# A transformer layer on one Trainium2 core: gate pieces one by one and context decays among the levels in the GLA heads, and column turns, squares and factors at other places in the opening

## The chip, the cores and the metric

The kernel runs on one core of one Trainium2 chip. The metric is the device time of one execution in microseconds (us), the median over runs on the chip. Before the change it is 1982.68 us in three runs (1981.75 to 1982.88).

Five engines take part: PE (TensorE, the matrix products), ACT (ScalarE), DVE (VectorE), POOL (GpSimd) and SP (SyncE, which only issues DMAs here). Each has its own instruction stream in a fixed order, and they wait for one another through semaphores.

## The reference, cut to what matters

One hybrid layer over 256 latent tokens and 256 context tokens, width 2048, all float32. Only what the change touches is shown: the modulated norm, the one input projection, and the gated linear attention (GLA) with 4 heads of key width 256 and value width 512.

```python
mod_x = jnp.split((silu(c) @ w_mod + b_mod), 6); mod_c = jnp.split((silu(c_ctx) @ w_mod + b_mod), 6)
h  = rms_norm(x, g_mix) * (1 + mod_x[1]) + mod_x[0]
hc = rms_norm(ctx, g_mix) * (1 + mod_c[1]) + mod_c[0]
qa, ka, va, qb, kb, vb, rb, lrf, lrb, gate_a, gate_b = split(h @ w_in)     # and of hc
gf = log_sigmoid(lrf @ w_gate_f + b_gate_f) / 16                           # gb likewise
...
def gla_final_state(k, v, g):                 # of the context, forward and flipped
    b = cumsum(g, axis=1)
    return einsum("bthd,bthe->bhde", k * exp(b[:, -1:] - b), v)
def gla_chunked(q, k, v, g, s0):              # of the latent tokens, both directions
    ...                                       # o_t = q_t exp(b_t) s0 + sum_{s<=t} (q_t . k_s exp(b_t - b_s)) v_s
```

After these come attention over a window and the context, the merge of both branches, the output projection and a convolutional feed-forward part. The change leaves them alone.

## The kernel before, in words

**Products.** Every large float32 product is made of three products of a shorter type: a weight tile `raw` (128 x 1024) is copied to `whi` on ACT (L207), the rest `wlo` is a difference on DVE (L208), and PE takes hi·hi, lo·hi and hi·lo (L83). Weights stream in once, on SP's queue, 0.5 MB a tile.

**The opening.** The modulation columns (shift and scale of the first norm) must be there before the first projection. `mod_both` makes them for a group of k-tiles: each `step` loads a 1 MB tile `mraw` and multiplies it into `pm` on PE (L95), the last step's transpose `mtr` runs on DVE (L324), and `end` has a small product `pcol` on PE and copies on DVE (L334). So each `end` has PE wait for a transpose that itself waits for PE. The groups are (first k-tile, number): (0,2), (2,2), (4,4), (8,4), (12,4). `square_sums` and `factor_row` make the norms' row factors, on ACT, PE (`pr`, L448) and DVE. `affine_scale` multiplies x by factor and scale on DVE (L488), `affine_shift` adds the shift and splits into `h..hi` on ACT (L495) and `h..lo` on DVE (L496). Latent tiles begin with h0, context tiles with h1. For each group the projections QB, KB and VB of all tokens are then taken over that group's k-tiles; the sums of the groups gather in `qb0`, `kbt` and `vb0`. Group 0's QB columns go to `qb0` by ACT copies (L503). From group 1 on, `mid` is called inside the projections and takes as many steps of the next group's columns from `bg_steps` as the list `steps` says; a finished column's `end` goes through `put` to a queue that the next tick empties, or is run at once.

**The GLA heads.** `with_gla` runs `gla_A`, a generator, beside a block of projection products (VB columns; KB columns in head 0). The block has 8 k-tile pairs, and the generator is called twice in each, 16 calls to a head: one before the 16 hi·hi and lo·hi products of a pair, one before its 8 products with `wlo`. A rate (0.91) says after how many calls it goes on to its next `yield`. One head has:

- four gate pieces (two directions, two halves of the head): one product `pz` on PE, four ACT instructions (L721 to L725), one add on DVE for the latent half (L726) and one on POOL for the context half (`gc`, L727). They are two to a step;
- a product `pa` of raw queries and keys, then eight levels. Level lv takes exponentials on ACT (L766, L767, L773, L774), multiplies them into `q2` and `k2` on DVE (L768, L775), and updates four running sums `segs` on DVE (L777 to L780). The product of a level (`pa`, L95, then a DVE L751 `COPY_PREDICATED` into `at`) is placed one step behind, so that the next level's vector work runs meanwhile;
- at the end the products with the context's decayed keys. The decays `kf` and `kg` are four scans of `gc` on DVE (L800, L802), a total `tot`, three exponentials on ACT and two multiplies with the context keys on DVE (L808, L809), all behind level 7 in the program. The final `pa` takes them with `q2`, `q3`.

The order on each engine follows the order of the program, with a scheduler that moves DVE and ACT work within it by readiness; `in_order(a, b)` holds b behind a.

Of the kernel before, what the change touches and what calls it, by code (L numbers as in the profile page):

```python
# [8 lines left out]
F32 = mybir.dt.float32  # L9
# [3 lines left out]
ALU = mybir.AluOpType  # L13
# [18 lines left out]
def layer_kernel(ctx, tc, A, out):  # L32
# [363 lines left out]
    def rms_scale(ss, n, shape):  # L396
# [15 lines left out]
    mods = [[mod_both(part, t0, n, dst, put) for part, dst in ((1, scale1), (0, shift1))]  # L412
            for (t0, n), put in zip(groups, [None, None] + 3 * [lambda fn: defer(0, fn)])]

# [4 lines left out]
    def square_sums(s):  # L419
# [3 lines left out]
        for i in range(4):  # L423
            x_ = xr[2 * s + i // 2][:, (i % 2) * 4:(i % 2) * 4 + 4, :]
            q = wr.tile([P, 4, T], F32, name="sq", tag="raw")
            if s + i:
                S.activation(q, x_, AF.Square)
            else:
                V.tensor_tensor(q, x_, x_, op=ALU.mult)
                parts.extend(q[:, k, :] for k in range(4))  # L430
                continue
            h = q[:, 0:2, :]
            V.tensor_tensor(h, h, q[:, 2:4, :], op=ALU.add)
            if s and whole is not None:
# [114 lines left out]
    hold_hi.extend([None, j])  # L549
    proj_T(w_in, QB, kts, [h_all(0)], add_to(lambda i: qb0[i], True))  # L550
    proj_T(w_in, QB + 512, kts, [h_all(0)], add_to(lambda i: qb0[2 + i], True))
    wk, wv = wsplit_raw(raws[0]), wsplit_raw(raws[1])
# [12 lines left out]
    affine_shift(1, *groups[0])  # L565
    ea()
    b0()
    b1()
    for s in range(2):
        affine_scale(s, *groups[1])  # L570
    early.extend([wk, wv])
    proj_T(w_in, KB, kts, [h_all(1)], lambda i, b: S.activation(half(i, T), pair_of(b), AF.Copy), mid=eb)
    i0, j0 = affine_shift(0, *groups[1])
    proj_nat(w_in, 0, VB, kts, [h_tok(1, 0), h_tok(1, 1)],
             lambda i, b: S.activation(vb0[:, 2 + i, :], b, AF.Copy))
    early.extend(wload(w_in[2 * P:4 * P, c:c + 512]) for c in (QB, QB + 512, KB, VB))
    hold.append(i0)
# [18 lines left out]
    for gi, (t0, n) in enumerate(groups):  # L596
# [8 lines left out]
        if gi + 1 < len(groups):  # L605
            bg_steps.extend(mods[gi + 1][0] + mods[gi + 1][1])
            ticks = 4 * ((n + 1) // 2)
            bg_rate[:] = [1.4 * len(bg_steps) / ticks + 0.01, 0.0]
            if gi == 1:
                bg_rate[:] = [0.0, 0.0]  # L610
                steps = iter([1, 2, 1, 2, 2, 0])

                def mid():
                    pin[0] = last[0]
                    for _ in range(next(steps)):
                        bg_steps.pop(0)()
                    pin[0] = None
        if t0 == 8:
            more_h(1)
        for s in range(2):  # L620
            if gi > 1:
                affine_scale(s, t0, n)
                affine_shift(s, t0, n)
            if s == 0:
# [80 lines left out]
    def gla_A(h, kb, qb, res):  # L705
# [7 lines left out]
        for d in range(2):  # L713
            g_ = W2("fc", "gc", [P, 2, T])
            for dt in range(2):
# [10 lines left out]
                V.tensor_tensor((PF if d == 0 else SB)[:, dt, :], mn[:, 0:T], e[:, 0:T], op=ALU.add)  # L726
                G.tensor_tensor(g_[:, dt, :], mn[:, T:2 * T], e[:, T:2 * T], op=ALU.add)  # L727
            gc.append(g_)
            yield

# [26 lines left out]
        for lv in range(8):  # L757
# [21 lines left out]
            V.tensor_tensor(pfR, pfR, pfL[:, :, m - 1:m].to_broadcast([P, n, m]), op=ALU.add)  # L779
            V.tensor_tensor(sbL, sbL, sbR[:, :, 0:1].to_broadcast([P, n, m]), op=ALU.add)  # L780
            if lv == 1:
                yield
            if lv:
                products(lv - 1, *prev)
            prev = q2, k2
            yield
        products(7, *prev)
# [9 lines left out]
        tot = sm.tile([P, 2], F32, name="tot", tag="tot", bufs=2)  # L797
        one = ones[:, 0:1].to_broadcast([P, T])
        for dt in range(2):
            V.tensor_tensor_scan(kf[:, dt, :], one, gc[0][:, dt, :], 0.0, op0=ALU.mult, op1=ALU.add)  # L800
            V.memset(kg[:, dt, 0:1], 0.0)
            V.tensor_tensor_scan(kg[:, dt, 1:T], ones[:, 0:1].to_broadcast([P, T - 1]), gc[1][:, dt, 0:T - 1], 0.0,  # L802
                                 op0=ALU.mult, op1=ALU.add)
        V.tensor_scalar(tot, kf[:, :, T - 1], -1.0 / 16, None, op0=ALU.mult)
        for dt in range(2):
            S.activation(kf[:, dt, :], kf[:, dt, :], AF.Exp, scale=1.0 / 16, bias=tot[:, dt:dt + 1])
        S.activation(kg, kg, AF.Exp, scale=-1.0 / 16)
        V.tensor_tensor(kf, kf, kc, op=ALU.mult)  # L808
        V.tensor_tensor(kg, kg, kc, op=ALU.mult)  # L809
        yield  # L810
# [507 lines left out]
```

## Time and profile before

| what | value |
|---|---|
| median of three runs | 1982.68 us (1981.75 to 1982.88) |
| the profiled execution | 1981.3 us |
| its span (first to last instruction) | 1979.5 us |
| mean granted TensorE clock | 0.999 |
| PE busy | 1955.1 us, 99% of the span |
| DVE busy | 1399.8 us, 71% |
| ACT busy | 972.1 us, 49% |
| POOL busy | 44.2 us, 2% |

The profile is of one execution. A line of a timeline has the start, the length, the engine, the program line, the operation with output and inputs, and how many like it follow; in brackets, how long the engine stood idle before it and what released it. A line of waits has the engine and its line, the engine and line that released it, the total in us, how often, and the longest. A line of windows has a stretch, its length, and then the busy time of each engine in it, the clock, and the busy share and rate of the DMA engines. In the trace each product of the columns (`pm`) counts as two matmuls, so `x4` in the program's order reads `x8` there.

### The profile page before, as it was taken

How to read it: one execution, taken by the hardware profiler on the slowest of the kernel's cores; microseconds unless marked ns; L12 is line 12 of the kernel's file. 1: busy time of each engine (PE TensorE's matmuls, PEld its weight loads, DVE VectorE, ACT ScalarE, POOL GpSimd, SP SyncE). 2: the span in 40 equal slices, each digit the busy share in tenths (PEclk: the TensorE clock that was granted, in tenths of full speed). 3: DMA queues.
4: the chain of work that ended last, by engine and by line, in shares of the span. 5: the costliest groups of instructions: out<-in, count | busy, mean ns of one | idle time of the engine just before them, and what ended most of it. 6: DMA issues, size and time to landing. Idle time of an engine off the chain costs nothing.

```text
span 1979.5 us, 27075 instructions
## 1 busy us (share of the span) xinstructions
PE 1955.1 (99%) x10292; PEld 1636.0 (83%) x10292; DVE 1399.8 (71%) x2150; ACT 972.1 (49%) x1415; POOL 44.2 (2%) x60
## 2 busy tenths in 40 slices
PE   7999999999999999999999999999999999999999
PEld 5679988888887778888888888888888888888887
DVE  5756767876767988777766467989886555677754
ACT  4323555552345666444444445755555334555533
POOL 0010010012000000000000000000000000000000
PEclk9999999999999999999999999999999999999999
DMA  9966222336754456888888677688886566666563
GB/s 379 413 258 185 75 85 78 93 108 205 233 160 118 127 181 213 268 290 292 289 286 265 235 236 262 198 271 285 257 274 228 193 197 188 187 190 189 188 216 109
DMA packets 183666, 420.88 MB, mean 213 GB/s; under 512 B 12544, under 2 KB 12768, under 8 KB 178800
## 3 DMA queue, kind: packets, MB, share of 16 engines
q1 hardware_dynamic: 182000, 413.45, 63.9%
q0 software_dynamic: 1360, 5.54, 1.0%
q8 instruction: 80, 1.31, 0.3%
q14 instruction: 50, 0.41, 0.1%
q10 hardware_dynamic: 176, 0.17, 0.0%
HBM read 416.98 MB, written 2.13 MB: 212 GB/s over the span
## 4 chain that ended last, share of the span: by engine, by line
PE 68%; DVE 0%; ACT 0%; issue 0%; DVEq 0%
PE acc L83 52%; PE accs L83 12%; PE poa L95 1%; PE pS L95 1%; PE ptp L98 1%; PE pto L98 0%; PE ptx L98 0%; DVE wlo L208 0%; ACT s L986 0%; PE ptq L98 0%; DVE s L991 0%; DVE yd L1238 0%; DVE yd L1232 0%; DVE raw L365 0%; ACT whi L207 0%
## 5 line engine op out<-in xcount | busy, mean ns | idle before, releaser
L208 DVE TENSOR_TENSOR wlo<-raw,whi 128x1024 fp32r<-128x1024 f32 x568 | 694.1, 1223 | 439.9 <-ACT whi L207 396.4
L207 ACT ACTIVATE whi<-raw 128x1024 fp32r<-128x1024 f32 x568 | 601.5, 1060 | 765.9 <-PE acc L83 608.9
L83 PE MATMUL accs<-h,whi 128*128 128x512 f32 x704 | 176.3, 392 | 0.0
L83 PE MATMUL acc<-h,whi 128*128 128x512 f32 x640 | 160.4, 392 | 0.0
L83 PEld LDWEIGHTS accs<-h,whi 128*128 128x128 f32 x704 | 126.6, 189 | 22.7
L83 PE MATMUL acc<-whi,h01hi 128*128 128x512 f32 x352 | 139.9, 398 | 0.0
L83 PE MATMUL acc<-whi,h00hi 128*128 128x512 f32 x352 | 138.9, 395 | 0.0
L83 PE MATMUL acc<-whi,h00lo 128*128 128x512 f32 x352 | 138.1, 392 | 0.0
L83 PE MATMUL acc<-whi,h01lo 128*128 128x512 f32 x352 | 137.8, 392 | 0.0
L83 PE MATMUL acc<-whi,ah 128*128 128x512 f32 x352 | 137.0, 389 | 0.0
L83 PE MATMUL acc<-whi,al 128*128 128x512 f32 x352 | 137.0, 389 | 0.0
L83 PEld LDWEIGHTS acc<-h,whi 128*128 128x128 f32 x640 | 115.0, 189 | 20.6
L83 PEld LDWEIGHTS accs<-h,wlo 128*128 128x128 f32 x704 | 96.0, 190 | 6.9
L83 PE MATMUL acc<-wlo,h01hi 128*128 128x512 f32 x352 | 98.7, 396 | 0.0
L83 PE MATMUL accs<-h,wlo 128*128 128x256 f32 x704 | 98.2, 282 | 0.0
L83 PE MATMUL acc<-wlo,h00hi 128*128 128x512 f32 x352 | 97.8, 394 | 0.0
L83 PE MATMUL acc<-wlo,ah 128*128 128x512 f32 x352 | 94.3, 389 | 0.0
L83 PEld LDWEIGHTS acc<-h,wlo 128*128 128x128 f32 x640 | 87.4, 190 | 6.3
L83 PE MATMUL acc<-h,wlo 128*128 128x256 f32 x640 | 89.4, 282 | 0.0
L365 DVE CUSTOM_DVE_ANT_0 raw<-raw,csrow,pack 128x1024 f32<-128x1024 f32 x64 | 81.4, 1281 | 0.0
L83 PEld LDWEIGHTS acc<-whi,ah 128*128 128x128 f32 x352 | 66.1, 188 | 13.7
L83 PEld LDWEIGHTS acc<-whi,al 128*128 128x128 f32 x352 | 66.1, 188 | 13.7
(377 smaller groups left out, 3558.1 us busy)
## 6 DMA issues: line engine op xcount, KB each, us to landing
raw<-in_w_in SPq DMA_DIRECT2D x208, 512.0 KB, 4.2
raw<-in_w_up SPq DMA_DIRECT2D x176, 512.0 KB, 4.1
raw<-in_w_modT SPq DMA_DIRECT2D x128, 512.0 KB, 4.4
raw<-in_w_down SPq DMA_DIRECT2D x88, 512.0 KB, 3.6
mraw<-in_w_mod SPq DMA_DIRECT2D x32, 1024.0 KB, 12.1
raw<-in_w_attn_o SPq DMA_DIRECT2D x32, 512.0 KB, 5.0
raw<-in_w_gla_o SPq DMA_DIRECT2D x32, 512.0 KB, 5.1
raw<-in_w_out SPq DMA_DIRECT2D x32, 512.0 KB, 4.7
```

The source lines that it names most:

```text
L83: r = pe_seq(PE.matmul(*a, **k))
L95: return pe_seq(after(PE.matmul(*a, **k)))
L98: return pe_seq(after(PE.transpose(*a)))
L207: j = S.activation(hi[:, 0:n, :], raw[:, 0:n, :], AF.Copy).ins
L208: i = V.tensor_tensor(lo[:, 0:n, :], raw[:, 0:n, :], hi[:, 0:n, :].bitcast(F32), op=ALU.subtract).ins
L365: i0 = V.tensor_tensor_reduce(out=raws[i], in0=raws[i], in1=row[0], scale=1.0, scalar=d if h else bmod[:, b0:b0 + 1], op0=ALU.mult, op1=AL ...
```

## The change

There are two parts.

In the GLA heads, `gla_A` yields after each of the four gate pieces, the extra yield in level 1 is gone, and the rate is 0.97. The decays (the same scans, total, exponentials and multiplies) move from behind level 7 into the levels: one half's scans behind level 2, the other's behind level 3, total and exponentials behind level 4, the multiplies behind level 6, each held behind the last `segs` add of that level. `kf` and `kg` get their buffers from the tag `fb` instead of `fa`.

In the opening, two of the context's squares are held behind ACT's copies of QB group by group; group 1's scale column ends later (`ea` behind `b0` and `b1`), the context's scaling of group 1 stands behind the VB products of the context; group 2's column ends go to a list `pend` and are run one at a time at set calls of `mid`; its last four steps are taken in one call; and the scaling of group 2 and the latent shift are placed in the calls too.

```diff
@@ opening
-            for (t0, n), put in zip(groups, [None, None] + 3 * [lambda fn: defer(0, fn)])]
+            for (t0, n), put in zip(groups, [None, None] + [lambda fn: pend.append(fn)] + 2 * [lambda fn: defer(0, fn)])]
+    pend = []
...
-                S.activation(q, x_, AF.Square)
+                j = S.activation(q, x_, AF.Square).ins
+                if s and i in (0, 2):
+                    in_order(evicted[i + 1], j)
...
+    evicted = []
+    for j in range(2):
+        proj_T(w_in, QB + j * 512, kts, [h_all(0)],
+               lambda i, b, j=j: evicted.append(S.activation(qb0[2 * j + i], b, AF.Copy).ins))
...
-    ea()
     b0()
     b1()
-    for s in range(2):
-        affine_scale(s, *groups[1])
+    ea()
+    affine_scale(0, *groups[1])
...
+    affine_scale(1, *groups[1])
     early.extend(wload(w_in[2 * P:4 * P, c:c + 512]) for c in (QB, QB + 512, KB, VB))
...
-                steps = iter([1, 2, 1, 2, 2, 0])
+                steps = iter([1, 2, 1, 4, 0, 0])
+
+                def next_columns():
+                    if pend:
+                        pend.pop(0)()
+
+                def scale_2():
+                    next_columns()
+                    for s in range(2):
+                        affine_scale(s, *groups[2])
+
+                also = iter([next_columns] * 3 + [scale_2, next_columns, lambda: affine_shift(0, *groups[2])])
 
                 def mid():
                     pin[0] = last[0]
+                    next(also)()
                     for _ in range(next(steps)):
                         bg_steps.pop(0)()
...
-            if gi > 1:
+            if gi > 2:
                 affine_scale(s, t0, n)
+            if gi > 2 or (gi == 2 and s):
                 affine_shift(s, t0, n)
@@ gla_A
                 G.tensor_tensor(g_[:, dt, :], mn[:, T:2 * T], e[:, T:2 * T], op=ALU.add)
+                yield
             gc.append(g_)
-            yield
+
+        kf = W2("fb", "kf", [P, 2, T])
+        kg = W2("fb", "kg", [P, 2, T])
+
+        def decays(dt, level):
+            one = ones[:, 0:1].to_broadcast([P, T])
+            i = V.tensor_tensor_scan(kf[:, dt, :], one, gc[0][:, dt, :], 0.0, op0=ALU.mult, op1=ALU.add).ins
+            V.memset(kg[:, dt, 0:1], 0.0)
+            j = V.tensor_tensor_scan(kg[:, dt, 1:T], ones[:, 0:1].to_broadcast([P, T - 1]), gc[1][:, dt, 0:T - 1],
+                                     0.0, op0=ALU.mult, op1=ALU.add).ins
+            in_order(level, i, j)
+
+        def decayed(level):
+            tot = sm.tile([P, 2], F32, name="tot", tag="tot", bufs=2)
+            in_order(level, V.tensor_scalar(tot, kf[:, :, T - 1], -1.0 / 16, None, op0=ALU.mult).ins)
+            for dt in range(2):
+                S.activation(kf[:, dt, :], kf[:, dt, :], AF.Exp, scale=1.0 / 16, bias=tot[:, dt:dt + 1])
+            S.activation(kg, kg, AF.Exp, scale=-1.0 / 16)
+
+        def decayed_keys(level):
+            in_order(level, V.tensor_tensor(kf, kf, kc, op=ALU.mult).ins)
+            in_order(level, V.tensor_tensor(kg, kg, kc, op=ALU.mult).ins)
+
+        beside_levels = {2: lambda i: decays(0, i), 3: lambda i: decays(1, i), 4: decayed, 6: decayed_keys}
...
-            V.tensor_tensor(sbL, sbL, sbR[:, :, 0:1].to_broadcast([P, n, m]), op=ALU.add)
-            if lv == 1:
-                yield
+            level = V.tensor_tensor(sbL, sbL, sbR[:, :, 0:1].to_broadcast([P, n, m]), op=ALU.add).ins
             if lv:
                 products(lv - 1, *prev)
             prev = q2, k2
+            if lv in beside_levels:
+                beside_levels[lv](level)
             yield
...
-        kf = W2("fa", "kf", [P, 2, T])
-        kg = W2("fa", "kg", [P, 2, T])
...
-        V.tensor_tensor(kf, kf, kc, op=ALU.mult)
-        V.tensor_tensor(kg, kg, kc, op=ALU.mult)
@@ with_gla
-        beside[:] = [gla_A(h, kb, qbt, res), 0.91, 0.0]
+        beside[:] = [gla_A(h, kb, qbt, res), 0.97, 0.0]
```

What the change moves is seen best in the order of instructions on two engines. First PE, in the opening, at the end of group 1's KB products, where group 2's columns are made (`pm_4` and `pcol_4`; a number behind a name tells one buffer from the next). Before:

```order
L83 MATMUL acc<-h10hi,wlo 128x256
L83 MATMUL acc<-h00hi,wlo 128x256
L83 MATMUL acc<-h10hi,wlo 128x256
L95 MATMUL pm_4_673<-mraw,cS 32x512 x8
L95 MATMUL pcol_4_724<-mtr,pack 32x32
L83 MATMUL acc<-whi,h00hi 128x512
L83 MATMUL acc<-whi,h00lo 128x512
```

With the change, the place 16 `wlo` products earlier:

```order
L83 MATMUL acc<-h10hi,whi 128x256
L83 MATMUL acc<-h10lo,whi 128x256
L95 MATMUL pcol_4_666<-mtr,pack 32x32
L95 MATMUL pm_4_683<-mraw,cS 32x512 x16
L83 MATMUL acc<-h00hi,wlo 128x256
L83 MATMUL acc<-h10hi,wlo 128x256
L83 MATMUL acc<-h00hi,wlo 128x256
```

All four steps of the second column stand ahead of the 16 `wlo` products, and its `pcol` behind them; before, half of the steps and the `pcol` followed the products directly. The first column's `pcol` had stood 32 products further up, directly behind its own last `pm`.

Second PE, in head 1, where the gate pieces are. Before:

```order
L95 MATMUL pz<-wgl 128x512 x2
L83 MATMUL acc<-wlo,h00hi 128x512 x4
L83 MATMUL acc<-wlo,h10hi 128x512 x4
L95 MATMUL pz<-wgl 128x512 x2
L83 MATMUL acc<-whi,h00hi 128x512
```

With the change:

```order
L95 MATMUL pz<-wgl 128x512
L83 MATMUL acc<-wlo,h00hi 128x512 x4
L83 MATMUL acc<-wlo,h10hi 128x512 x4
L95 MATMUL pz<-wgl 128x512
L83 MATMUL acc<-whi,h00hi 128x512
```

The other two `pz` follow at the next two calls, behind the 16 `whi` and the next 8 `wlo` products; the first level product stands one call later than before, the products of levels 6 and 7 and the final one stand where they stood.

Third DVE, in the same head, at its end. Before:

```order
L794 TENSOR_TENSOR q_3133<-q_3133,qb 128x512
L62 TENSOR_TENSOR ats<-at,ats 128x256
L800 SCALAR_TENSOR_TENSOR kf<-ones,gc 128x256
L801 MEMSET kg 128x1
L802 SCALAR_TENSOR_TENSOR kg<-ones,gc 128x255
L62 TENSOR_TENSOR ats<-pa,ats 128x256
L800 SCALAR_TENSOR_TENSOR kf<-ones,gc 128x256
L801 MEMSET kg 128x1
L802 SCALAR_TENSOR_TENSOR kg<-ones,gc 128x255
L208 TENSOR_TENSOR wlo<-raw,whi 128x1024
L804 TENSOR_SCALAR tot<-kf 128x2
L809 TENSOR_TENSOR kg<-kg,kb_109 128x512
```

With the change the first two scans stand here, behind level 2:

```order
L821 TENSOR_TENSOR segs<-segs 128x64x4
L822 TENSOR_TENSOR segs<-segs 128x64x4
L793 COPY_PREDICATED at<-lmask,pa 128x256
L754 SCALAR_TENSOR_TENSOR kf<-ones,gc 128x256
L755 MEMSET kg 128x1
L208 TENSOR_TENSOR wlo<-raw,whi 128x1024
L756 SCALAR_TENSOR_TENSOR kg<-ones,gc 128x255
L810 TENSOR_TENSOR q_2955<-q_2955,qb 128x512
```

The scans, the total and the two multiplies (L768 and L769 now) have left the end of the head and stand ahead of DVE's work for levels 3, 4, 5 and 7. DVE's `wlo` and all other work keep their number.

More of the change, by code (lines that the diff above doesn't have):

```diff
@@ L549, in layer_kernel @@
     hold_hi.extend([None, j])
-    proj_T(w_in, QB, kts, [h_all(0)], add_to(lambda i: qb0[i], True))
-    proj_T(w_in, QB + 512, kts, [h_all(0)], add_to(lambda i: qb0[2 + i], True))
+    evicted = []
+    for j in range(2):
+        proj_T(w_in, QB + j * 512, kts, [h_all(0)],
+               lambda i, b, j=j: evicted.append(S.activation(qb0[2 * j + i], b, AF.Copy).ins))
     wk, wv = wsplit_raw(raws[0]), wsplit_raw(raws[1])
@@ L794, in gla_A @@
             V.tensor_tensor(dst, dst, q_, op=ALU.mult)
-        kf = W2("fa", "kf", [P, 2, T])
-        kg = W2("fa", "kg", [P, 2, T])
[L797 to L809, printed above, removed]
         yield
```

## The prediction, made before the changed kernel was run

> **What bounds the kernel now.** I read the page's totals first, then the waits of PE in the two places that the diff touches, then the timeline and the windows around each wait.
>
> ```profile
> span 1979.5 us, 27075 instructions
> PE 1955.1 (99%) x10292; PEld 1636.0 (83%) x10292; DVE 1399.8 (71%) x2150; ACT 972.1 (49%) x1415; POOL 44.2 (2%) x60
> ```
>
> PE is busy for all but 24.4 us of the span. The change removes no product, so it can only gain where PE waits, or where it starts late behind a wait. The first view is PE's waits from 24 to 75 us, the second the same from 205 to 460 us, the four GLA heads.
>
> ```profile
> PE pcol L95 <- DVE mtr L324: 2.6, 4, 0.8
> PE acc L83 <- ACT h10hi L495: 0.7, 1, 0.7
> PE acc L83 <- ACT h00hi L495: 0.4, 1, 0.4
> PE acc L83 <- ACT qb L503: 0.4, 1, 0.4
> PE acc L83 <- DVE h10lo L496: 0.2, 1, 0.2
> ```
>
> ```profile
> PE pa L95 <- DVE q L768: 3.1, 4, 1.1
> PE pa L95 <- DVE kf L808: 2.5, 3, 1.0
> ```
>
> All that can be had is there: 4.3 us in the opening, 5.6 us in the heads. A wait costs somewhat more than its row, because the last products before it run out unhidden. The rows of group 2's columns show it:
>
> ```profile
> 60.35 1.07 PE L95 MATMUL pm<-mraw,cS 128*32 128x512 f32 x8
> 62.26 0.25 PE L95 MATMUL pcol<-mtr,pack 128*32 128x32 f32 x2 [0.84 <-DVE mtr L324]
> ...
> 66.45 1.92 PE L95 MATMUL pm<-mraw,cS 128*32 128x512 f32 x16
> 68.30 0.39 PE L83 MATMUL acc<-h00hi,wlo 128*128 128x256 f32 x1
> ...
> 70.40 1.92 PE L95 MATMUL pm<-mraw,cS 128*32 128x512 f32 x16
> 73.16 0.25 PE L95 MATMUL pcol<-mtr,pack 128*32 128x32 f32 x2 [0.84 <-DVE mtr L324]
> 73.34 0.50 PE L83 MATMUL acc<-whi,h00hi 128*128 128x512 f32 x1
> ```
>
> Sixteen take 1.92 us and eight 1.07, so eight more cost 0.85: a group that is followed by a wait pays 1.07 - 0.85 = 0.22 us for its tail. The seven waits in the opening that the change touches (all but `h00hi`) are then worth at most 4.3 - 0.4 + 7 x 0.22 = 5.4 us, and the seven in the heads 5.6 + 7 x 0.22 = 7.1 us. That is the ceiling, 12.5 us.
>
> **The opening, part by part.** No arithmetic is added or removed. The edits and what each takes away: the context's squares behind ACT's QB copies lift the `qb` wait of 0.4 us; `ea` behind `b0` and `b1` puts 16 column products over the first of group 1's two `pcol` waits (2.6 - 2 x 0.84 = 0.9 us between them); the context's scaling of group 1 moved back frees DVE, and with it the `h10` waits of 0.7 and 0.2; group 2's ends, run a call later, lie behind 32 and 16 products instead of directly behind their own last `pm`, and the two waits of 0.84 us go. The cover of the last is the 16 products with `wlo`, 2.1 us (68.30 to 70.40), against the 0.84 that the transpose takes beyond PE's work now; without it the 0.84 would be back. So for PE alone the gain is near the ceiling, about 5 us.
>
> But PE is not alone here. The next view is windows of 10 us in the opening; the last two columns are the DMA engines' share and rate.
>
> ```profile
> 40.00:50.00 10.00, 8.21 (x83) 5.91 (x76) 7.44 (x27) 3.47 (x8) 0.00 (x0) 1.00 1.05 404
> 60.00:70.00 10.00, 9.16 (x76) 6.50 (x75) 7.16 (x20) 0.00 (x0) 0.00 (x0) 1.00 1.02 417
> 100.00:110.00 10.00, 10.00 (x84) 9.03 (x83) 4.36 (x5) 1.06 (x1) 0.00 (x0) 1.00 0.99 391
> 110.00:120.00 10.00, 10.00 (x53) 8.39 (x52) 4.87 (x13) 3.61 (x6) 0.00 (x0) 1.00 0.15 59
> ```
>
> Until 110 us the loads run without a gap at about 400 GB/s, so data cannot come earlier, however early PE asks. The order of the loads does not change. Where PE would overtake them is found by the landing of each tile `mraw` of group 2's last column; the tile's own view, narrowed to one issue at a time, gives issue and time to landing:
>
> ```profile
> L104 SPq DMA_DIRECT2D mraw<-in_w_mod x1: 328/328/328, 55.4 to 55.4; - x1
> DMA to landing us min/median/max: 10.0/10.0/10.0
> ...
> L104 SPq DMA_DIRECT2D mraw<-in_w_mod x1: 328/328/328, 58.5 to 58.5; - x1
> DMA to landing us min/median/max: 9.4/9.4/9.4
> ```
>
> They land at 65.4 and 67.9 us, 2.5 apart. The change takes all four steps of this column before the 16 `wlo` products. PE, ahead by the waits removed so far (about 3 us), comes to the fourth step near 66.5 and stands until 67.9. From there: the fourth step 0.93, the 16 `wlo` products 2.1, `pcol` 0.2: the VB products begin at 71.1 instead of 73.34. **The opening gives 2.2 us**, not 5. Could even this be lost later, since the stream is full to 110 us? The other weights land 2.5 us or more before their use as I read their landings, and beyond 110 us the loads have a gap (share 0.15), so I keep 2.2. The bounds: 0, if the stream also sets the pace behind 73 us, and 5.
>
> The Trainium skill has a rule that speaks against keeping it: "Perfetto Trace Analysis", section "Identifying the Most-Contended Engine", says to find the most-contended engine and to optimise that first. In the opening it is DMA, and by this rule freeing PE of waits there would bring 0, the second rival below. The trace agrees on which is busiest, with the shares of 1.0 above, and disagrees for 100 to 110 us, where PE is busy all the time.
>
> **The heads.** No work is added or removed here either: the same four scans, total, exponentials and two multiplies. What moves on DVE is priced by these rows, grouped by form in the window of the heads, and by the spacing of starts in a timeline of head 1's end:
>
> ```profile
> L802 DVE TENSOR_TENSOR_SCAN kg<-ones,gc 128x255 f32<-128x255 f32 x8 | 5.5, 683 | 0.0
> L800 DVE TENSOR_TENSOR_SCAN kf<-ones,gc 128x256 f32<-128x256 f32 x8 | 5.5, 683 | 3.4 <-PE pa L95 3.4
> L808 DVE TENSOR_TENSOR kf<-kf,kb 128x512 f32<-128x512 f32 x4 | 2.8, 688 | 0.4 <-ACT kf L806 0.4
> ```
>
> ```profile
> 318.70 0.69 DVE L800 TENSOR_TENSOR_SCAN kf<-ones,gc 128x256 f32<-128x256 f32 x1
> 319.31 0.68 DVE L802 TENSOR_TENSOR_SCAN kg<-ones,gc 128x255 f32<-128x255 f32 x1
> 322.62 0.69 DVE L809 TENSOR_TENSOR kg<-kg,kb 128x512 f32<-128x512 f32 x1
> 323.75 0.69 DVE L808 TENSOR_TENSOR kf<-kf,kb 128x512 f32<-128x512 f32 x1 [0.45 <-ACT kf L806]
> ```
>
> A scan takes 0.61 us from start to start, a multiply about 0.6, the total 0.1: 4 x 0.61 + 2 x 0.6 + 0.1 = 3.8 us a head, which leave the end, where the final product waits for them, and go in among the levels. Is there room? Windows of head 1, from its first gate piece to the first product's wait, from there to the last level, and from there to the final product, and the level stretches of heads 2 and 3:
>
> ```profile
> 274.59:289.52 14.93, 13.86 (x65) 11.14 (x64) 8.69 (x14) 12.88 (x22) 4.69 (x4) 1.00 0.28 80
> 289.52:317.54 28.02, 28.02 (x148) 23.24 (x149) 26.56 (x55) 13.59 (x34) 0.00 (x0) 1.00 0.36 108
> 317.54:324.59 7.05, 6.51 (x33) 5.24 (x32) 6.46 (x14) 3.66 (x8) 0.95 (x1) 1.00 0.12 18
> 353.30:380.87 27.57, 27.56 (x148) 23.52 (x149) 27.11 (x56) 13.45 (x32) 0.80 (x1) 1.00 0.31 88
> 417.77:445.55 27.78, 27.78 (x149) 23.48 (x150) 27.34 (x56) 12.62 (x31) 0.00 (x0) 1.00 0.45 134
> ```
>
> In the level stretches DVE is busy 26.6 of 28.0, 27.1 of 27.6 and 27.3 of 27.8 us (third busy figure of each row): no room for 3.8 us. That is the argument against the change. For it speaks the first row: until the first product, ACT has 12.9 of 14.9 us, the four gate pieces piled up in two calls, and DVE only 8.7. One piece a call brings the pieces' results evenly, and the first product, one call later now, no longer waits:
>
> ```profile
> 289.52 1.16 PE L95 MATMUL pa<-q,kb 128*128 128x128 f32 x8 [1.07 <-DVE q L768]
> ```
>
> I followed head 1 through with the new order of its instructions and the spacings above. The last gate add is done near 287.5 us as before; the first product comes on time (1.07 + 0.22 gained). Then DVE has 29.7 us to do before the operands of the last level, where it had 25.9 (the 3.8 more), so it passes that point at 317.3 at the earliest, and with small waits the last level is at 317.7 to 318.5, up to 1.0 late against 317.54. Behind it nothing is left that the final product needs but `q2`, `q3`: its wait, the 0.54 us by which PE's 6.51 falls short of 7.05, goes with its tail, and the final product begins between 323.2 and 323.9 instead of 324.59. **Head 1 gains 1.0 us.** The same count gives 0.8, 0.5 and 0.7 for heads 0, 2 and 3; they differ by how much of the streaming work (`wlo`, L365) falls into the levels. **The heads give 3.0 us.**
>
> The bounds: upwards all waits gone, 7.1. Downwards each head pays its 3.8 us of backlog in full and gets back only the two waits with tails, about 2.0: 1.8 a head, 7.2 us slower in all. A side effect goes with the decays' new buffers (tag `fb`): the scans' own wait of 3.4 us on `pa` in the row above goes; DVE has other work then, so I give it no value of its own.
>
> The other price in this stretch is POOL beside DVE. The gate add of the context half is on POOL, and it slows what DVE does with two tensors at that time:
>
> ```profile
> L727 POOL TENSOR_TENSOR gc<-gm,ge x16: 746/974/1711, 213.8 to 416.4; 128x256 f32<-128x256 f32 x16
> L726 DVE TENSOR_TENSOR segs<-gm,ge x16: 424/426/966, 213.7 to 414.9; 128x256 f32<-128x256 f32 x16
> L768 DVE TENSOR_TENSOR q<-q,qb x32: 677/684/1570, 223.3 to 443.4; 128x512 f32<-128x512 f32 x32
> ```
>
> The longest are 966 against 424 ns and 1570 against 677. The change keeps the sixteen POOL adds, and the last one of a head now ends nearer to the first multiply; I take no change. The Trainium skill, "SBUF — State Buffer", section "SBUF: two separate sides", says that the port shared by GpSimd and VectorE is held for a whole instruction and that the other side stops; the longest rows agree with it. By this rule the last add, moved up against the first multiply, would cost each head up to 1570 - 684 = 0.89 us once more, and the sum of the heads would come near 0; that is close to the third rival below.
>
> **The sum.** Against the profiled execution's 1981.3 us (span 1979.5 and 1.8 around it): -2.2 - 3.0 = -5.2, so 1976.1. The median of the runs shown is 1982.7, 1.4 above that execution: **1977.5 us**. A change below 0.2%, 4.0 us, cannot be told from none here, so faster means below 1978.7 and slower above 1986.6.
>
> **The rivals.**
> - All waits of the heads go (DVE catches up because the scans fill its remaining gaps): -2.2 - 7.1 = -9.3, 1973.4 us. For it: DVE's slack of 1.5 us in head 1's levels. Against: only 0.5 us of slack in heads 2 and 3.
> - The stream of loads sets the pace of the whole opening, which gives nothing: -3.0, 1979.7 us. For it: a share of 0.99 to 1.05 in the windows up to 110 us. Against: PE's busy 10.00 of 10.00 from 100 to 110 us, so there it was PE that set the pace.
> - The heads give nothing: the time won at the first product is lost again at levels 4 to 7: -2.2, 1980.5 us.
> - Slower: the decays among the levels become DVE's backlog, and products behind level 3 wait for `q2` and `k2`. The place is PE's `pa` in calls 10 to 14 of each head; the price is 1.8 us a head, +7.2 - 2.2 = +5.0, 1987.7 us. It decides from the point where the backlog at the last level is more than what the head recovers, 2.0 us; my own count has 1.0 for head 1. For it: the three level windows above. Against: the first product's wait and the end's spare time.
>
> **How the numbers follow.** Forecast 0.52 (faster 0.46, same 0.06); all waits gone 0.12, all faster; the stream 0.08 (faster 0.02, same 0.06); heads neutral 0.13 (faster 0.02, same 0.11); backlog 0.15 (slower 0.13, same 0.02). Faster 0.62, same 0.25, slower 0.13. The forecast's own range is 1974.5 to 1980.0, down by four times the 0.8 us between 317.7 and 318.5, up to just short of the third rival. For 8 in 10 it has to reach the first rival at 1973.5 and half way into the last: 1973.5 to 1985.0.
>
> **What would show it.** In the profile after: the four `pcol` waits and the `qb` wait gone, a new wait of PE for a load `mraw` of about 1.4 us at 66 to 68 us, the VB products of group 1 near 71.2. In the heads: the waits for `q` at the first products gone, waits for `q` or `k` at levels 4 to 7 of a few tenths, none for `kf`, and DVE's level stretches at 98% or more. I am wrong if PE's waits for DVE in the heads exceed 5.6 us in sum, or if a wait appears where the first load of group 2 is used.

## The result, and the profile after

The changed kernel takes 1976.03 us (median of seven runs, 1975.74 to 1976.17); the kernel before takes 1981.75 in the same session (1980.98 to 1983.28). The ratio is 0.9970, with a 95% interval of 0.9959 to 0.9981: 5.7 us faster. The prediction was 5.2 us faster, 1977.5 us. The spans of the two profiled executions differ by 5.2 us. The page after:

```profile
span 1974.3 us, 27051 instructions
PE 1951.2 (99%) x10292; PEld 1634.6 (83%) x10292; DVE 1398.5 (71%) x2150; ACT 971.2 (49%) x1415; POOL 38.9 (2%) x60
```

Every engine counts the same number of instructions as before, so the work is the same. PE's busy time fell by 3.9 us and its idle time by 1.3, so the page's totals do not say where the gain is: the products in front of a wait count as busy while they run out, and in the profile before PE ran at half clock for 3.4 us of the opening (the rows are in "The opening taken apart"). PE's waits and the starts of its products say it. PE's waits from 24 to 75 us, the opening (what waits, for what: us in total, times, longest):

```profile
PE pm L95 <- DMA mraw<-in_w_mod: 3.9, 4, 1.6
PE acc L83 <- ACT h00hi L498: 0.5, 1, 0.5
```

and from 200 to 460 us, the four heads:

```profile
PE pa L95 <- DVE k L817: 3.6, 4, 1.1
```

In the opening the waits for DVE's transposes, for the QB copies and for `h10` are gone, and in their place PE waits for the loads of `mraw`. In the heads the waits for `q` at the first products and for `kf` at the end, 5.6 us together, are gone, and 3.6 us for `k` in the levels have come. The opening in PE's timeline after:

```profile
42.34 0.85 PE L95 MATMUL pm<-mraw,cS 128*32 128x256 f32 x12 [1.64 <-DMA mraw<-in_w_mod]
...
65.78 1.07 PE L95 MATMUL pm<-mraw,cS 128*32 128x512 f32 x8 [0.29 <-DMA mraw<-in_w_mod]
68.27 1.07 PE L95 MATMUL pm<-mraw,cS 128*32 128x512 f32 x8 [1.42 <-DMA mraw<-in_w_mod]
...
71.36 0.25 PE L95 MATMUL pcol<-mtr,pack 128*32 128x32 f32 x2
71.54 0.50 PE L83 MATMUL acc<-whi,h00hi 128*128 128x512 f32 x1
```

The last load is awaited for 1.42 us. Its issue and its time to landing:

```profile
L104 SPq DMA_DIRECT2D mraw<-in_w_mod x1: 328/328/328, 56.6 to 56.6; - x1
DMA to landing us min/median/max: 11.6/11.6/11.6
```

It lands at 68.2, and the VB products begin at 71.54 instead of 73.34: 1.8 us earlier. From then on I matched the two traces' products. Those behind the heads start 4.9 us earlier, so the heads brought 3.1, and the rest of the span 0.3. By head, from the first `pz` to the first final product, counted with PE's loss (the distances from start to start, less what the same products take back to back; worked out from the trace):

| kernel | head 0 | head 1 | head 2 | head 3 | all |
|---|---|---|---|---|---|
| before | 2.20 | 3.65 | 2.94 | 3.55 | 12.3 |
| changed | 1.40 | 2.27 | 2.27 | 3.81 | 9.8 |

Head 3 lost more than before. The experiments start from there.

### The profile page after: what moved, and what is told of

It is laid out like the page before. It is cut to its first block, busy times and chain, and to the rows that moved or that the text cites. A ratio compares the mean times of both kernels' runs of the same rounds, so it can differ in the third digit from the quotient of the medians.

```text
span 1974.3 us, 27051 instructions
## 1 busy us (share of the span) xinstructions
PE 1951.2 (99%) x10292; PEld 1634.6 (83%) x10292; DVE 1398.5 (71%) x2150; ACT 971.2 (49%) x1415; POOL 38.9 (2%) x60
## 4 chain that ended last, share of the span: by engine, by line
PE 94%; DVE 3%; DMA 2%; ACT 1%; issue 0%; SPq 0%; DVEq 0%; ACTq 0%
PE acc L83 72%; PE accs L83 12%; DMA mraw<-in_w_mod 2%; PE pa L95 2%; PE poa L95 1%; PE pS L95 1%; PE po L95 1%; PE pm L95 1%; PE ptp L98 1%; DVE wlo L208 1%; PE pto L98 0%; DVE q L810 0%; DVE k L817 0%; DMA pack<-in_k_pack 0%; PE ptq L98 0%
## 5 line engine op out<-in xcount | busy, mean ns | idle before, releaser
L365 DVE CUSTOM_DVE_ANT_0 raw<-raw,csrow,pack 128x1024 f32<-128x1024 f32 x64 | 81.4, 1279 | 0.0
```

Source lines behind the costliest of these rows:

```text
L365: i0 = V.tensor_tensor_reduce(out=raws[i], in0=raws[i], in1=row[0], scale=1.0, scalar=d if h else bmod[:, b0:b0 + 1], op0=ALU.mult, op1=AL ...
```

## The experiments

Each run is set against the kernel before, timed beside it on the same chip. The median of that kernel was 1981.3 to 1981.5 there, and its runs spread from 1980.65 to 1983.42. Differences below are medians against that, in us.

### The parts alone

The opening's edits without the heads' (all of the diff's parts up to `gla_A`), and the heads' without the opening's.

> Only the opening's edits, heads as before. My theory: the VB products of group 1 begin 1.8 to 2.2 us earlier and all of it reaches the end: 1.8 us faster (1.3 to 2.4), with the same waits of PE for mraw as in the changed kernel (3.9 us in four). Rival (the load stream sets the pace of the whole opening): 0, the start of the heads at the place of before, 209.6 us. Rival (the parts need each other): more or less than 1.8 by over 0.8.

> Only the heads' edits, opening as before. My theory: 3.1 to 3.7 us faster, the heads' own waits as in the changed kernel (3.6 us for k, none for q at the first product, none for kf), and this run and the one with the opening alone sum to the change's 5.2 in the profiled spans within 0.6. Rival: a sum off by more than 1 us, if an earlier end of the opening is what lets the heads gain.

The opening alone takes 1979.21 us: 2.25 faster, ratio 0.9986 (0.9977 to 0.9995). The heads alone take 1978.27: 3.2 faster, ratio 0.9985 (0.9976 to 0.9993). The sum is 5.4, the whole change gives 5.7. So the gain of the opening is carried to the end, although the loads take the DMA engines' whole time there, and the parts add. The heads' waits are those of the changed kernel: 3.6 us for `k`, no others.

Then the two halves of the heads' edit, with the old opening. In the first the diff is only

```diff
+                yield
             gc.append(g_)
-            yield
...
-            if lv == 1:
-                yield
...
-        beside[:] = [gla_A(h, kb, qbt, res), 0.91, 0.0]
+        beside[:] = [gla_A(h, kb, qbt, res), 0.97, 0.0]
```

and in the second these lines are as before, and `decays`, `decayed` and `decayed_keys` stand in the levels.

> Heads with the four gate pieces one to a call and the decays where they were. My theory: the first products no longer wait (four waits, 3.1 us and tails, 4.0 together), the end's wait for kf stays at 2.5 us or some tenths more: 2.5 to 4.0 us faster, that is about as good as both edits together. Rival (the decays' place brings the gain): less than 1.5 us faster, because the levels then start one call later and the final product waits as much longer.

> Heads with the decays among the levels and the gate pieces two to a call as before. My theory: the first products wait as before (3.1 us), the kf wait goes (2.5 us and tails, about 3.2), but 3.8 us of VectorE work a head meet 0.4 to 1.5 us of room in the levels, so new waits of 1 to 2 us a head appear at levels 3 to 7: between 1 us faster and 4 us slower, middle 1.5 slower. Rival (VectorE catches up): 2.5 to 3.5 us faster, no new wait in the levels.

The pieces alone take 1976.92 us, 4.5 faster, ratio 0.9975 (0.9966 to 0.9985). That is more than both halves together, and more than the 2.5 to 4.0 that were expected. The decays alone take 1982.38, 0.9 slower in the median, ratio 1.0004 (0.9995 to 1.0013), not told from no change. PE's waits in the heads, first of the pieces alone:

```profile
PE pa L95 <- DVE kf L806: 2.8, 3, 1.2
PE pa L95 <- DVE k L775: 0.4, 1, 0.4
```

then of the decays alone:

```profile
PE pa L95 <- DVE k L799: 3.4, 8, 0.9
PE pa L95 <- DVE q L792: 2.5, 4, 1.1
```

The pieces take away the waits for `q` and leave those for `kf` as they were. The decays' move takes away those for `kf`, 2.5 us, and puts 3.4 us for `k` in their place. So the change's gain in the heads is the gate pieces' 4.5 us, and with the other half 1.3 of them are lost again. What of the move costs this is the question of the next part.

> The change without the move of the decays (opening and gate pieces only). My theory now: the two parts add, 2.25 and 4.5 us as measured alone, so about 6.7 us faster than before and 1.2 us faster than the whole change. Rival (the decays' move costs only where the opening is the old one): as fast as the whole change, 5.4 to 5.7.

Opening and pieces, without the decays' move, take 1974.84 us (1974.77 to 1975.06), 6.5 faster than before, ratio 0.9968 (0.9955 to 0.9980). The runs of the changed kernel all lie above 1975.7. The price of the move holds with the new opening too.

### Where the price of the decays sits

Head 3 of the changed kernel was the suspect. First its decays went back to the end, in head 3 alone:

```diff
-        beside_levels = {2: lambda i: decays(0, i), 3: lambda i: decays(1, i), 4: decayed, 6: decayed_keys}
+        beside_levels = {2: lambda i: decays(0, i), 3: lambda i: decays(1, i), 4: decayed, 6: decayed_keys} if h < 3 else {}
...
+        if h == 3:
+            decays(0, level)
+            decays(1, level)
+            decayed(level)
+            decayed_keys(level)
         yield
         yield
```

Second, the streaming columns (L365) were kept out of head 3, by a rate of 0 there:

```diff
         beside[:] = [gla_A(h, kb, qbt, res), 0.97, 0.0]
+        if h == 3:
+            bg_rate[:] = [0.0, 0.0]
```

> The whole change, but head 3 keeps its decays at the end. My theory: the price of the move sits in head 3, where VectorE also has the streaming columns (L365) among the levels; its waits for k at levels 3 to 7 go, its wait for kf comes back: PE's loss in head 3 from 3.8 to about 2.3 us, the kernel about 1.3 us faster than the whole change, 7.0 faster than before. Rival (the price is spread over the heads): as the whole change, 5.4 to 5.9.

> The whole change with no streaming columns (L365) in head 3; their work follows behind the heads. My theory: three of them, 1.2 us each, leave the levels, head 3's loss falls from 3.8 to 1.5 to 2.3 us: 6.9 to 7.8 us faster than before, if the stretch behind takes them at no cost. Rival (it is POOL's work beside VectorE, 10 us in that window, that slows head 3): the loss stays above 3 us and the time within 0.5 of the whole change.

With head 3's decays at the end the kernel takes 1974.15 us (1973.91 to 1974.73), 7.2 faster than before, ratio 0.9964 (0.9952 to 0.9977): the best of all that were run, and ahead of both kernels. PE's loss in head 3 is 2.0 us instead of 3.8. So the place is head 3. The columns are not cleared by their run: with the rate at 0 only one of the three left head 3 (two still ran there, at 431.37 and 443.63 us). The loss stays at 3.5, and the work, pushed behind the heads, costs there: 1976.47 us, 4.8 faster than before. Its theory missed, and the rival that it named, POOL's work, came out by both of its signs: the loss is above 3 us, and the time is within 0.5 of the whole change.

What else is in head 3? POOL's timeline of the changed kernel, 424 to 450 us (first and last rows):

```profile
426.90 0.54 POOL L916 DMA_DIRECT2D rope<-in_k_rope  x1 [13.87 <-DVE kg L755]
429.99 0.54 POOL L924 TENSOR_TENSOR att<-rope,norms 128x128 f32<-128x128 f32 x1 [2.54 <-DMA rope<-in_k_rope]
...
436.03 0.96 POOL L926 TENSOR_TENSOR att<-rope,norms 128x64 f32<-128x64 f32 x2
```

and of the kernel before:

```profile
451.44 0.54 POOL L889 DMA_DIRECT2D rope<-in_k_rope  x1 [33.80 <-DVE kg L801]
455.69 0.45 POOL L897 TENSOR_TENSOR att<-rope,norms 128x128 f32<-128x128 f32 x1 [3.70 <-DMA rope<-in_k_rope]
```

The load of `rope` takes a buffer of the tag that `gc` has, and POOL waits until DVE has scanned head 3's `gc`. With the scans 25 us earlier POOL's twelve table products for the attention run at 430 to 437 us, in the middle of head 3's levels, instead of behind them. This is DVE there, two multiplies and two adds of level 5:

```profile
433.18 0.80 DVE L810 TENSOR_TENSOR q<-q,qb 128x512 f32<-128x512 f32 x1
433.90 0.94 DVE L817 TENSOR_TENSOR k<-k,kb 128x512 f32<-128x512 f32 x1
434.76 0.53 DVE L819 TENSOR_TENSOR segs<-segs 128x256 f32<-128x256 f32 x1
435.21 0.54 DVE L820 TENSOR_TENSOR segs<-segs 128x256 f32<-128x256 f32 x1
```

To test it, the load of `rope` was to come after the head. The first try ordered the load behind head 3's last split:

```diff
+    ends = []
...
+        ends[:] = [split(atc[0], atc[1], pa)]
...
-    G.dma_start(rope, A["k_rope"])
+    with tc.issue_after(ends[0]):
+        G.dma_start(rope, A["k_rope"])
```

> The whole change, with the load of rope held until head 3's last split is done, so that POOL's table products cannot run beside head 3's levels. Theory A (the early decays of head 3 set a buffer free that POOL waited for, and POOL's products slow VectorE in the levels): PE's loss in head 3 falls from 3.8 to 2.0 to 2.6 us, the time by 1.2 to 1.8 below the whole change, 6.9 to 7.5 us faster than before. Rival (the backlog of the decays alone, with the streaming columns): the loss stays above 3.2 us and the time within 0.5 of the whole change.

It takes 1975.77 us (1975.63 to 1975.95) and settles nothing: the load still went out at 426.90 us, and the order of the instructions on PE, DVE, ACT and POOL is that of the changed kernel. The statement made no engine wait for another; the run is a second measure of the changed kernel. The second try gives POOL something to wait for, an add that reads head 3's last operand `q3` and writes into the tile of `rope` ahead of the load:

```diff
+    ends = []
...
+        ends[:] = [q3]
...
     rope = W2("fc", "rope", [P, 2, 2, P])
+    G.tensor_tensor(rope[:, 0, 0, :], ends[0][:, 0, 0:P], ends[0][:, 1, 0:P], op=ALU.add)
     G.dma_start(rope, A["k_rope"])
```

> The whole change, with a true wait this time: POOL first adds two halves of head 3's last q operand into the tile of rope, so the load of rope and the table products come after head 3's levels. In the run before this one the hold did not act: the load still went out at 426.9 us, and the theory was not tested. Theory A (POOL's products slow VectorE in head 3's levels; in the changed kernel's timeline the VectorE instructions from 429.8 to 436.7 us take 1.8 us more than the same forms elsewhere): PE's loss in head 3 falls by 1.2 to 1.8, from 3.8 to 2.0 to 2.6 us, and the time to about 1974.5. Rival (the backlog of the decays alone): the loss stays above 3.2 us, the time within 0.5 of 1976.0.

1974.43 us (1974.30 to 1975.00): 7.0 faster than before, ratio 0.9964 (0.9950 to 0.9977), 1.6 below the changed kernel and 1.3 below the run just before, without an overlap of the runs. PE, DVE and ACT have the changed kernel's order. POOL and DVE in it, the same instructions:

```profile
448.69 0.57 POOL L920 DMA_DIRECT2D rope<-in_k_rope  x1 [0.30 <-POOL rope L919]
```

```profile
432.22 0.69 DVE L812 TENSOR_TENSOR q<-q,qb 128x512 f32<-128x512 f32 x1
432.82 0.69 DVE L819 TENSOR_TENSOR k<-k,kb 128x512 f32<-128x512 f32 x1
433.43 0.42 DVE L821 TENSOR_TENSOR segs<-segs 128x256 f32<-128x256 f32 x1
433.76 0.42 DVE L822 TENSOR_TENSOR segs<-segs 128x256 f32<-128x256 f32 x1
```

The multiplies start 0.6 apart and not 0.7, and the adds take 0.42 and not 0.54. In all, DVE's instructions from 429.8 to 436.7 us in the changed kernel take 1.7 us more than the median of their forms in the heads. PE, first the changed kernel (the second product of head 3 that waits, and the final one), then this one (the only product of head 3 that waits, and the final one):

```profile
434.98 1.13 PE L95 MATMUL pa<-q,k 128*128 128x128 f32 x8 [1.08 <-DVE k L817]
448.61 0.59 PE L95 MATMUL pa<-q,kf 128*128 128x256 f32 x2
```

```profile
428.71 1.13 PE L95 MATMUL pa<-q,k 128*128 128x128 f32 x8 [0.52 <-DVE k L819]
446.90 0.59 PE L95 MATMUL pa<-q,kf 128*128 128x256 f32 x2
```

In the changed kernel that product waits 1.08 us for `k`; here only the one before it waits, 0.52, as it does in the changed kernel too. The head's first `pz` starts 0.2 us earlier here, the final product 1.7: the loss in head 3 falls from 3.8 to 2.3, and theory A stands. The columns stayed in their places here, so they were not what cost the 1.5 us. The four heads together then lose about 8.2 us, as much as with opening and pieces alone: with POOL out of the way the decays' move costs nothing in the heads, and it gains nothing either.

### A better place for the scans?

If the levels are full, the slack before the first product may take the scans. Opening and pieces as in the change, the forward scans between the third and fourth gate piece, the exponentials of `kf` in level 1, `kf` and `kg` from the tag `fb`. The exponential of `kg` and the two multiplies, which the expectation has in the levels, stand at the end in the program:

```diff
+                if d and dt:
+                    kf = W2("fb", "kf", [P, 2, T])
...
+                    for x in range(2):
+                        V.tensor_tensor_scan(kf[:, x, :], one, gc[0][:, x, :], 0.0, op0=ALU.mult, op1=ALU.add)
```

The backward scans stand at the end in the program, but with their own buffers the scheduler takes them up beside the last gate piece too.

> Opening and gate pieces of the change; the four scans and the total stand between the gate pieces, where VectorE has room, the exponentials and multiplies (1.2 us) in levels 1 and 2. My theory: the levels are too full for 3.8 us but not for 1.2, so neither the end waits for kf (2.8 us) nor levels 3 to 7 wait: 8 to 10 us faster than before. Rival (the scans delay the last gate add, and with it the first product): a new wait for q of about 1 us a head at the first product, 5 to 7 us faster.

1977.18 us, 4.1 faster than before, ratio 0.9980 (0.9971 to 0.9989): the rival. PE's waits in the heads:

```profile
PE pa L95 <- DVE q L794: 3.7, 4, 1.2
PE pa L95 <- DVE k L801: 1.5, 1, 1.5
```

The scans stand ahead of the last gate add, and every first product waits again, 0.8 to 1.2 us. The wait for `k` is in head 3, where POOL's table products come at 419 to 428 us, with the early scans again. By head the loss is not even: against opening and pieces it is 1.1 us more in head 0 and 1.9 more in head 3, and 0.1 and 0.4 less in heads 1 and 2, where the end no longer waits for `kf`. So the run does not show that the place is a bad one; with POOL held back it was not run.

### The opening taken apart

The squares alone, as in the diff's second and third part, the rest as before:

> Only the context's squares held behind ACT's QB copies, all else as before. My theory: of the opening's 2.25 us this edit gives 0.4 to 1.0 on average, and it gives the steadiness: the runs spread over 0.5 us or less, as with the whole opening, where before they spread over 2.8, because the squares wait for the context's load and hold the copies up by 0.4 to 2.1 us from execution to execution. Rival (PE then waits for mraw instead, at 39 to 43 us): 0 in the median, and the spread remains.

1979.81 us, 1.5 faster in the median, ratio 0.9993 (0.9984 to 1.0002), so by its interval not told from none. The runs spread from 1979.08 to 1980.97, 1.9 us, not 0.5. The gain is above what was expected, the steadiness is not there: the lower six of its eleven runs (1979.08 to 1979.81) lie about where the opening as a whole has its own (1979.00 to 1979.38), the others 1 us or more above. PE's wait for `qb` is gone in the profiled run. That wait varies; here is ACT in the profile of before, then in the kernel with the decays alone, which has the same opening:

```profile
28.11 1.06 ACT L427 ACTIVATE sq<-xr 128x1024 f32<-128x1024 f32 x1 [0.91 <-DMA xr<-in_ctxT]
31.30 1.07 ACT L503 ACTIVATE qb<-acc 128x512 f32<-128x512 f32 x2
```

```profile
28.67 1.06 ACT L427 ACTIVATE sq<-xr 128x1024 f32<-128x1024 f32 x1 [2.66 <-DMA xr<-in_ctxT]
31.85 1.06 ACT L503 ACTIVATE qb<-acc 128x512 f32<-128x512 f32 x2
```

The squares stand in ACT's queue ahead of the QB copies and wait for the context's load, and PE waits for the copies: 0.4 us in the first profile, 2.1 in the second. The load's part in the difference is the 0.55 us between the two copies. The rest is when PE gets there. PE's product behind the wait, before, with the pieces alone (its copies start at 31.34, like those of before) and with the decays alone:

```profile
31.93 0.38 PE L83 MATMUL acc<-h00hi,whi 128*128 128x256 f32 x1 [0.41 <-ACT qb L503]
31.96 0.39 PE L83 MATMUL acc<-h00hi,whi 128*128 128x256 f32 x1 [1.38 <-ACT qb L503]
32.48 0.58 PE L83 MATMUL acc<-h00hi,whi 128*128 128x256 f32 x1 [2.15 <-ACT qb L503]
```

In the profile before, PE came to it 1 us late, because the granted clock (the column behind POOL's) was at half for 3.4 us. With the decays alone the clock went to half right behind the long wait, and PE stayed 2.0 us behind the profile of before. Both as windows:

```profile
20.20:23.40 3.20, 3.13 (x22) 1.49 (x22) 0.45 (x1) 1.06 (x1) 0.00 (x0) 0.50 1.05 389
32.40:35.70 3.30, 3.22 (x15) 3.22 (x16) 3.18 (x5) 3.30 (x6) 0.00 (x0) 0.50 1.03 429
```

Eight of the fourteen profiles have one such stretch of half clock, each between 20 and 46 us. Where a wait follows that PE would have stood in anyway, it costs nothing. That is what the other edits of the opening add. In all eight profiles with the whole opening and the four steps in one call, the VB products begin 3.3 us after the landing of the last `mraw`, wherever in 67.8 to 68.4 us that is, with a half-clock stretch (four of them) or without; with the old opening or the squares alone it is 4.6 to 7.1 us. The wait for the last load takes up what PE lost ahead of it.

Last, the wait of 1.42 us for the last `mraw`: with opening and pieces, the fourth step one call later.

```diff
-                steps = iter([1, 2, 1, 4, 0, 0])
+                steps = iter([1, 2, 1, 3, 1, 0])
...
+                def shift_2():
+                    next_columns()
+                    affine_shift(0, *groups[2])
-                also = iter([next_columns] * 3 + [scale_2, next_columns, lambda: affine_shift(0, *groups[2])])
+                also = iter([next_columns] * 3 + [scale_2, next_columns, shift_2])
```

> Opening and gate pieces as in the change (the decays at the end); the fourth step of group 2's last column is taken one call later, behind the 16 wlo products, and its end one call after that. My theory: PE no longer stands 1.4 us for the last mraw, and the column is still early enough for group 2: 0.5 to 1.4 us faster than opening and pieces as they are (1974.84). Rival (the load stream sets the pace): the wait appears again at group 2's first products, 0 to 0.5 slower.

1975.07 us (1974.19 to 1975.99) against 1974.84 for opening and pieces: no gain in the median. The wait at 68 us is gone, a smaller one stands at group 2's first products:

```profile
78.18 0.39 PE L83 MATMUL acc<-h00hi,whi 128*128 128x256 f32 x1 [0.20 <-ACT h00hi L498]
```

This profiled execution also lost 1.5 us at 42 to 46 us, ahead of the edit, in a half-clock stretch, but had caught up with opening and pieces by the VB products. Matched product by product it is 0.1 us ahead of them up to 77 us and 0.7 behind from group 2's first products on. So nothing of the 1.42 came back, and the rival's sign, 0 to 0.5 slower, fits the medians; but the row there names ACT's `h00hi` and no load, and the runs of the two kernels overlap. What sets the pace at 78 us is left open.

## Why the prediction came out as it did

- **The opening, 2.2 us.** Right in size and in what sets it: 1.8 in the change's profile by the start of the VB products, 2.25 alone in the medians. PE overtook the loads, as forecast, and stood 1.42 us at the last `mraw` (1.4 forecast). The VB products began 0.4 later than the 71.1 forecast, 0.3 of it because the load landed at 68.2 and not at 67.9; from landing to VB products it took 3.3 us, as in the forecast's sum. The parts on the way were mis-sized: the `qb` wait was priced at 0.4 us and its tail, from a profile in which PE came late to it. Against the profile of the pieces alone, with the old opening and full clock, the changed kernel is 1.8 us ahead at 33 us already, where of all its edits only the squares' place has acted, 2.7 at 64 us, and 1.8 at the VB products. So the column turns and the other edits won 0.9, and the wait for the load took it back. Not foreseen were the waits of 0.5 and 1.64 us for group 1's `mraw` near 40 us. The rival that the stream sets the pace of the whole opening fell. In the Trainium skill, "Perfetto Trace Analysis", section "Identifying the Most-Contended Engine", the advice is to optimise the most-contended engine first, with DMA judged by the use of the HBM and not by the share of its engines, which the prediction took; here 2.25 us came from waits of another, up to the landing of the load that PE then waits for.
- **The heads, 3.0 us.** Right as a sum: 3.1 in the profile, 3.2 alone in the medians. The parts of the sum were off. The first products' waits went, as said. The decays were counted as part of the gain, since the wait for `kf` ends, and as up to 1.0 us late at the last level. Measured, the pieces give 4.5 and the move takes 1.3 of it back. That the sum came out at 3.0 is in part luck: heads 1 and 2 were forecast 1.0 too low together, and head 3 0.9 too high.
- **The place of the backlog.** The prediction put it at the last level; it is at level 4, at the product of 302 us in head 1, which waited 1.00 us for `k` behind both pairs of scans, and the last level waited for nothing. By head the gains, matched product by product, were 0.8, 1.5, 1.0 and -0.2 where 0.8, 1.0, 0.5 and 0.7 were forecast. The place is the one that the backlog rival named, products behind level 3.
- **The step that failed** is in the part on POOL: "I take no change". The adds of `gc` did cost nothing new. But the price of POOL beside DVE, read from those adds, was not asked of what the scans release: a buffer, and with it POOL's products for the attention. That cost head 3 1.5 us and turned its gain into a small loss. The Trainium skill's rule in "SBUF — State Buffer", section "SBUF: two separate sides", that GpSimd and VectorE shut each other out of a shared port, was weighed at the first product, where nothing came of it. In head 3 the trace agrees with it in kind: DVE's adds shown above took 0.53 and 0.54 us instead of 0.42.
- **The backlog rival** had the right place, and for head 3 the right sign. Its size was far off: it had the heads 7.2 us slower, and they are 3.1 faster. The waits in the heads are 3.6 us, below the 5.6 named as the limit.
- **Why 5.7 and not 5.2, and 1976.0 and not 1977.5.** The two profiled executions differ by 5.2 us, as forecast. The changed kernel's profiled execution is at the median of its runs (1976.05 and 1976.03). That of before, 1981.3, is 0.45 below the median of the seven runs, and that is the 0.5. The forecast's time added 1.4 for the median of three runs, 1982.68; two of the three lie high in the spread of that kernel (1980.98 to 1983.28), so the 1.5 by which the time was too high comes from those runs and from no step of the mechanism.
- **A slip in the range.** Four times 0.8 us below 1977.5 is 1974.3, not 1974.5. Nothing hangs on it here.

## What to carry to other kernels

Work moved to an earlier place frees its buffers earlier too: look at what waits for them, on every engine, and what that will run beside. An edit of two halves is worth running as halves: here one half paid for the other, and the sum hid it. A queue entry that waits for a load should not stand ahead of copies that PE needs, even if the profile at hand shows a small wait there: it was 0.4 us in one profile and 1.4 to 2.1 in three others, according to when PE came.

## What the runs showed of the hardware that was not expected

POOL's table products (128x64 and 128x128, float32), about 7 us of them from 430 to 437 us, slowed DVE by 0.1 to 0.3 us in a `segs` add and 0.1 to 0.3 in a multiply. The same 128x64 product took 322 to 1303 ns there, and 313 to 1303 in the kernel before, behind the heads. With POOL held back, PE's loss in head 3 fell by 1.5 us and the kernel's time by 1.6.

The granted TensorE clock fell to 0.50 for one stretch of 3.4 us in eight of the fourteen profiles, at 20, 32 or 42 us, each time beside a wait of PE of 1.4 us or more; profiles with such waits and without the stretch are there too. It put PE back by about 1 us at 20 us and by 1.5 at 42. Where a later wait took that up, the time did not show it. Where none did, it stayed: in the kernel with the squares alone, whose profiled run is 1.2 us above its median, and in that with the decays alone, where the stretch comes at 32 us, behind the `qb` wait, and the profiled run is 1.8 us above its median.

In the eight kernels where the landing of a load sets the start of the VB products, the runs of each spread by 0.3 to 0.9 us; in the four with the old opening by 1.6 to 2.8.
